# Moving GpSimd's two-operand arithmetic to VectorE in a two-layer hybrid diffusion block

## The chip, the cores and the metric

The kernel runs on one core of a Trainium2 chip. A core has TensorE (PE, with its weight loads shown apart as PEld), VectorE (DVE), ScalarE (ACT), GpSimd (POOL) and SyncE (SP), each with a queue of its own that runs strictly in order, and DMA queues. The metric is the device time of one execution in microseconds (us), the median of several runs. A profiled execution is one more run, with its own time.

## What is computed

Two layers over 512 latent tokens and 256 context tokens of width 1024. Each layer projects its input to four token mixers (grouped-query attention with 2-D rotary, neighbourhood attention, Fourier mixing, a complex diagonal state-space scan), normalizes and joins them, projects them out, and runs a SwiGLU:

```
h = _rmsnorm(x, g_norm1) * (1.0 + sc1) + sh1
aq, ak, av, dq, dk, dv, fin, sin_ = _split_proj(h @ w_in)
...
o_a, oc_a = _gqa_mixer(aq, ak, av, caq, cak, cav, att_q_gain, att_k_gain, rope, need_ctx)
o_d, oc_d = _na_mixer(dq, dk, dv, cdq, cdk, cdv, na_q_gain, na_k_gain, na_rel_bias, need_ctx)
o_f = _fourier_mixer(fin, w_fourier)
o_s, oc_s = _s5_mixer(sin_, csin, ssm_lam_re, ssm_lam_im, ssm_log_dt, ssm_b_re, ssm_b_im,
                      ssm_c_re, ssm_c_im, ssm_d, w_glu, b_glu, need_ctx)
o = _group_norm(jnp.concatenate([o_a, o_d, o_f, o_s.astype(o_a.dtype)], axis=-1), g_group)
x = x + ga1 * (o @ w_out)
h2 = _rmsnorm(x, g_norm2) * (1.0 + sc2) + sh2
x = x + ga2 * _swiglu(h2, w_ff1, w_ff3, w_ff2)
```

The rotary step multiplies each head's halves by cosines and sines. The state-space mixer's powers of a_bar and its products with B and C are made on the chip as tables.

## The kernel before

Tokens lie on the free axis, channels on the 128 partitions. All large products are made in three matmuls from halves in fp32r: a weight tile `raw` (128x1024 f32, or 128x768 for the value projection) comes by a DMA on SP's queue, ScalarE casts it to `hi`, and GpSimd takes `lo = raw - hi` (`weights`, L222 to L235). `mm3` (L237) then adds hi times hi, hi times lo, and lo times hi, in that order. There are four buffers of `hi`, four of `lo` and two of `raw`; a buffer comes free when TensorE has done with its weights, or for `raw`, when both halves are made. 178 such tiles go through in one execution.

The order of the work on each engine is set by a scheduler that plays the program against a timeline of its own; weights stand at high priority. Each engine's queue then holds that order, and an instruction at its head that waits holds up all that stands behind it.

Stages, by the profile's time axis: from 0 to about 143 us the first layer's state-space tables (`tables`, L424 to L680: small DVE steps on tiles `sm`, then per m and direction the tiles `bg`, `bd`, `ot`, `o`, `gt`, `g`, and the rotation table `ro`, L661 to L666), its modulation and norm (`norm_apply`, L320, tiles `xa`, `h`) and its first projections; from 143 to 255 us rotary (`rope`, L914) and the scan (`s5`, L707, tiles `zt`, `hst`); to 450 us attention and Fourier; to 1065 us the output projection and the feed-forward (`dense`, L1261), which near its end, from 850 us, also makes the tables of the second layer; to 1145 us the norm between the layers; to 1295 us projections and scan of the second layer; to 1430 us its attention; and to 1834 us its output projection and feed-forward.

In the feed-forward each of 22 slices f takes two weight tiles (w1 and w3), silu on ScalarE, a product on DVE (`sg`, L1332) and a split into `gh` (ScalarE) and `gl` (DVE, L1337). After every three or four slices `down` adds their product with w2 to x (`update`, L1248). The psum tiles `psD` of these products are two in layer one, four in layer two.

In the tables GpSimd makes one product of every pair that DVE then adds or subtracts (`q2`, `q3`, `o2` as tile `o`, `g2` as tile `g`), one-operand copies (L594, L668), memsets and the loads `sbg`, `sbd`, `scd` of layer one. In `rope` GpSimd multiplies by the cosines. GpSimd's queue also issues DMAs of `s5` and of the Fourier part.

Of the kernel before, what the change touches and what calls it, by code (L numbers as in the profile page):

```python
# [18 lines left out]
P = 128  # L19
D = 1024  # L20
KT = 8
SEQ = 512
# [26 lines left out]
C_COS, C_SIN = 461, 973  # L49
# [134 lines left out]
class _Core:  # L184
# [37 lines left out]
    def weights(self, src, shape):  # L222
        nc = self.nc
        n = int(np.prod(shape))
        with self.tc.high_priority():
            hi = self.whi.tile([P, n], F32R, name="hi")
            raw = self.raw.tile([P, n], F32, name="raw")
            lo = self.wlo.tile([P, n], F32R, name="lo")
            pat = " ".join("abcd"[:len(shape)])
            nc.sync.dma_start(raw, src.rearrange(f"p {pat} -> p ({pat})") if len(shape) > 1 else src)  # L230
            nc.scalar.copy(hi, raw)  # L231
            nc.gpsimd.tensor_sub(lo, raw, hi)  # L232
        if len(shape) == 1:
            return hi, lo
        return tuple(t.rearrange("p (a b) -> p a b", b=shape[1]) for t in (hi, lo))  # L235
# [188 lines left out]
    def tables(self, l, tp, t2, role, nm, gate=None):  # L424
        nc, a = self.nc, self.a
        v, gp = nc.vector, nc.gpsimd
# [109 lines left out]
        for k in (1, 2, 4):  # L536
            o = slice(k + 1, 2 * k + 1)
            br, bi = (pw[:, i, k:k + 1].broadcast_to([P, k, M]) for i in range(2))
# [17 lines left out]
        ng = 16 // nm  # L556
# [3 lines left out]
        for m in range(nm):  # L560
# [3 lines left out]
            for d in range(2):  # L564
                with self.tc.issue_after(gate(m, d).ins) if gate and gate(m, d) else ExitStack():
# [4 lines left out]
                    def rev(ap):  # L570
                        return ap[:, ::-1] if d == 1 else ap

                    sbg = t2.tile([P, 2, np2, 16], F32, name="sbg", bufs=sb)
                    ld.dma_start(sbg, a["sbg"][:, :, q, ps2])
                    sbd = t2.tile([P, 2, ng, 16], F32, name="sbd", bufs=sb)
# [4 lines left out]
                    q2 = t2.tile([P, 2, np2, 16], F32, name="q2")  # L580
                    f8r, f8i = (t[:, c8].unsqueeze(2).broadcast_to([P, np2, 16]) for t in (fr, fi))
                    v.tensor_mul(bg[:, 0], sbg[:, 0], f8r)
                    gp.tensor_mul(q2[:, 0], sbg[:, 1], f8i)
                    v.tensor_mul(bg[:, 1], sbg[:, 1], f8r)
                    gp.tensor_mul(q2[:, 1], sbg[:, 0], f8i)
                    v.tensor_sub(bg[:, 0], bg[:, 0], q2[:, 0])
                    v.tensor_add(bg[:, 1], bg[:, 1], q2[:, 1])
                    bd = t2.tile([P, ng, 2, 16], F32, name="bd")
                    q3 = t2.tile([P, ng, 16], F32, name="q3")
                    f6r, f6i = (t[:, c16].unsqueeze(2).broadcast_to([P, ng, 16]) for t in (fr, fs))  # L590
                    v.tensor_mul(bd[:, :, 0], sbd[:, 0], f6r)
                    gp.tensor_mul(q3, sbd[:, 1], f6i)
                    v.tensor_add(bd[:, :, 0], bd[:, :, 0], q3)
                    gp.tensor_copy(bd[:, :, 1], bd[:, :, 0])  # L594
                    ot = t2.tile([P, ng, 9, 16], F32, name="ot", tag="w", bufs=wb)
# [1 line left out]
                    for dst, ci in ((ot, 0), (o2, 1)):  # L597
                        pv = rev(p12[:, ci, :, c16]).rearrange("p s g -> p g s").unsqueeze(3)
                        cv = scd[:, ci].unsqueeze(2)
                        (v if ci == 0 else gp).tensor_tensor(dst, pv.broadcast_to([P, ng, 9, 16]),  # L600
                                                             cv.broadcast_to([P, ng, 9, 16]), op=ALU.mult)
                    v.tensor_add(ot, ot, o2)
                    osl = ot[:, :, 0:8] if d == 1 else ot[:, :, 1:9]
# [14 lines left out]
                    else:  # L618
# [5 lines left out]
                    pr, pi = (rev(pw[:, i, 0:8, c8]).rearrange("p s g -> p g s").unsqueeze(3).broadcast_to(shp)  # L624
                              for i in range(2))
                    br, bi = (bg[:, i].unsqueeze(2).broadcast_to(shp) for i in range(2))
                    g2 = t2.tile(shp, F32, name="g2")
                    v.tensor_mul(gt[:, 0], pr, br)
                    gp.tensor_mul(g2, pi, bi)
                    v.tensor_sub(gt[:, 0], gt[:, 0], g2)  # L630
                    g3 = t2.tile(shp, F32, name="g3")
                    v.tensor_mul(gt[:, 1], pr, bi)
# [281 lines left out]
    def rope(self, t):  # L914
        nc = self.nc
        sw = self.xn.tile([P, NT], F32, name="xn")
        nc.vector.stream_shuffle(sw[:, :SEQ], t[:, :SEQ], list(range(16, 32)) + list(range(16)))
        nc.gpsimd.tensor_mul(t[:, :SEQ], t[:, :SEQ], self.cst[:, C_COS:C_COS + SEQ])
        nc.vector.tensor_mul(sw[:, :SEQ], sw[:, :SEQ], self.cst[:, C_SIN:C_SIN + SEQ])
        nc.vector.tensor_add(t[:, :SEQ], t[:, :SEQ], sw[:, :SEQ])  # L920

# [531 lines left out]
```

## Time and profile before

| | us |
|---|---|
| median of 3 runs | 1827.36 (1827.08 to 1835.4) |
| the profiled execution | 1835.55, of which span 1833.8 |
| TensorE busy | 1725.8 (94%) |
| VectorE busy | 969.5 (53%) |
| ScalarE busy | 527.2 (29%) |
| GpSimd busy | 558.6 (30%) |

Times in the rows below are microseconds from the span's start. A busy TensorE counts matmuls that are pipelined, with modelled ends. "a <- b" in a list of waits means that a waited and that b's end released it. In the chain of work each step is followed back to what released it.

### The profile page before, as it was taken

How to read it: one execution, taken by the hardware profiler on the slowest of the kernel's cores; microseconds unless marked ns; L12 is line 12 of the kernel's file. 1: busy time of each engine (PE TensorE's matmuls, PEld its weight loads, DVE VectorE, ACT ScalarE, POOL GpSimd, SP SyncE). 2: the span in 40 equal slices, each digit the busy share in tenths (PEclk: the TensorE clock that was granted, in tenths of full speed). 3: DMA queues.
4: the chain of work that ended last, by engine and by line, in shares of the span. 5: the costliest groups of instructions: out<-in, count | busy, mean ns of one | idle time of the engine just before them, and what ended most of it. 6: DMA issues, size and time to landing. Idle time of an engine off the chain costs nothing.

```text
span 1833.8 us, 25688 instructions
## 1 busy us (share of the span) xinstructions
PE 1725.8 (94%) x10142; PEld 1395.3 (76%) x10142; DVE 969.5 (53%) x2259; ACT 527.2 (29%) x852; POOL 558.6 (30%) x360
## 2 busy tenths in 40 slices
PE   5899999898999999999899998989999999999999
PEld 2667877566878888888678877778767787787887
DVE  7988535572177445446956346265666632232332
ACT  2422234452241211121121223323444432222221
POOL 4553200201221322231643512423111244344442
PEclk7999989999999999999899998989999999999999
DMA  8355340414135434343342332332322123233222
GB/s 337 103 155 165 128 167 24 167 53 182 38 125 151 127 127 153 107 154 110 106 110 75 106 112 81 132 110 89 114 64 64 47 92 93 77 107 103 93 92 81
DMA packets 83065, 207.25 MB, mean 113 GB/s; under 512 B 15360, under 2 KB 35968, under 8 KB 82816
## 3 DMA queue, kind: packets, MB, share of 16 engines
q1 hardware_dynamic: 54160, 160.44, 26.9%
q0 software_dynamic: 7824, 29.38, 4.8%
q10 hardware_dynamic: 20960, 15.78, 2.8%
q8 instruction: 80, 1.31, 0.3%
q14 instruction: 41, 0.34, 0.1%
HBM read 185.68 MB, written 21.99 MB: 113 GB/s over the span
## 4 chain that ended last, share of the span: by engine, by line
PE 76%; DVE 15%; issue 4%; ACT 2%; POOL 1%; DMA 1%; ACTq 0%; DVEq 0%; POOLq 0%
PE psD L241 54%; PE psD L703 4%; PE psS L932 3%; PE psT L241 2%; PE psQ L979 1%; PE psQ L990 1%; PE psT L376 1%; PE psS L801 1%; POOL lo L232 1%; PE psT L856 1%; PE psQ L1045 1%; DVE ro L662 1%; PE psQ L1030 1%; PE psT L278 1%; PE psT L1067 1%
## 5 line engine op out<-in xcount | busy, mean ns | idle before, releaser
L232 POOL TENSOR_TENSOR lo<-raw,hi 128x1024 fp32r<-128x1024 f32 (+1 forms) x178 | 432.2, 2434 | 875.5 <-ACT hi L231 875.2
L241 PE MATMUL psD<-big,hi 128*128 128x512 f32 (+1 forms) x2368 | 605.9, 360 | 12.2 <-ACT big L331 5.7
L241 PEld LDWEIGHTS psD<-big,hi 128*128 128x128 f32 x2368 | 399.8, 191 | 88.1 <-ACT big L331 8.1
L231 ACT CAST hi<-raw 128x1024 fp32r<-128x1024 f32 (+1 forms) x178 | 184.2, 1039 | 774.5 <-PE psD L241 466.6
L241 PE MATMUL psD<-big,lo 128*128 128x512 f32 (+1 forms) x1184 | 368.2, 359 | 1.2 <-POOL lo L232 1.2
L241 PEld LDWEIGHTS psD<-big,lo 128*128 128x128 f32 x1184 | 202.9, 191 | 38.4 <-POOL lo L232 2.7
L1332 DVE TENSOR_TENSOR sg<-sg,psD 128x768 f32<-128x768 f32 (+1 forms) x44 | 36.1, 820 | 308.8 <-PE psD L241 300.5
L241 PE MATMUL psD<-gh,hi 128*128 128x512 f32 (+1 forms) x528 | 163.6, 359 | 4.9 <-DVE xb L1248 4.7
L241 PE MATMUL psD<-gl,hi 128*128 128x512 f32 (+1 forms) x528 | 165.8, 360 | 0.0
L241 PE MATMUL psD<-gh,lo 128*128 128x512 f32 (+1 forms) x528 | 163.6, 358 | 0.0
L1248 DVE SCALAR_TENSOR_TENSOR xb<-psD,mod,xb 128x512 f32<-128x512 f32 (+1 forms) x112 | 64.7, 613 | 114.9 <-PE psD L241 114.8
L1337 DVE TENSOR_TENSOR gl<-sg,gh 128x768 fp32r<-128x768 f32 (+1 forms) x44 | 99.2, 2254 | 39.5 <-ACT gh L1335 39.5
L407 DVE CUSTOM_DVE_ANT_0 junk<-wmt,cb,pcol 128x1024 f32<-128x1024 f32 x64 | 97.1, 1517 | 27.3 <-DMA wmt<-in_wmodT 26.2
L241 PEld LDWEIGHTS psD<-gh,hi 128*128 128x128 f32 x528 | 89.5, 189 | 24.4 <-DVE xb L1248 8.5
L241 PEld LDWEIGHTS psD<-gh,lo 128*128 128x128 f32 x528 | 90.1, 189 | 16.6 <-issue 0.2
L241 PEld LDWEIGHTS psD<-gl,hi 128*128 128x128 f32 x528 | 89.8, 189 | 15.8 <-issue 0.4
L1248 DVE SCALAR_TENSOR_TENSOR xq<-psD,mod,xq 128x512 f32<-128x512 f32 (+1 forms) x64 | 42.2, 682 | 78.6 <-PE psD L241 78.6
L932 PE MATMUL psS<-k,q 64*128 64x256 f32 (+1 forms) x432 | 78.2, 336 | 3.4 <-DVE mx L1019 3.0
L241 PE MATMUL psD<-h,hi 128*128 128x512 f32 (+1 forms) x288 | 76.2, 350 | 4.2 <-ACT h L331 2.7
L932 PEld LDWEIGHTS psS<-k,q 64*128 64x128 f32 x432 | 58.1, 195 | 23.6 <-issue 9.1
L241 PEld LDWEIGHTS psD<-h,hi 128*128 128x128 f32 x288 | 50.7, 194 | 15.4 <-ACT h L331 3.2
L241 PE MATMUL psD<-on,hi 128*128 128x256 f32 (+1 forms) x176 | 51.6, 331 | 1.3 <-ACT on L1081 1.3
(396 smaller groups left out, 2494.5 us busy)
## 6 DMA issues: line engine op xcount, KB each, us to landing
raw<-in_w_ff SPq DMA_DIRECT2D x132, 512.0 KB, 3.5
wmt<-in_wmodT SPq DMA_DIRECT2D x48, 512.0 KB, 3.6
wm<-in_wmod SPq DMA_DIRECT2D x28, 512.0 KB, 6.0
raw<-in_winT SPq DMA_DIRECT2D x18, 512.0 KB, 3.6
room<-in_wmod SPq DMA_DIRECT2D x12, 512.0 KB, 11.4
nab<-in_nab SPq DMA_DIRECT2D x8, 640.0 KB, 4.2
rot<-trot POOLq DMA_DIRECT2D x8, 576.0 KB, 6.0
cf<-in_four POOLq DMA_DIRECT2D x8, 520.0 KB, 4.9
```

The lines of the kernel that those rows point to most:

```text
L231: nc.scalar.copy(hi, raw)
L232: nc.gpsimd.tensor_sub(lo, raw, hi)
L241: nc.tensor.matmul(o, lhsT=lhs[i], rhs=rhs[j][..., s], start=start and n == 0, stop=stop and n == 2)
L278: self.nc.tensor.matmul(dst, lhsT=src, rhs=self.ident, start=True, stop=True)
L376: nc.tensor.matmul(ps[32 * j:32 * j + 32], lhsT=self.cvec[:, k], rhs=ws[k // 2][:, k % 2], start=half == 0, stop=half == 1)
L407: nc.vector.tensor_tensor_reduce(junk, w, cb[:, i], 1.0, self.pcol[1][:, PC_B + f:PC_B + f + 1], op0=ALU.mult, op1=ALU.add, accum_out=mod[ ...
L662: v.tensor_mul(er[:, :, :, o], er[:, :, :, s], bcr)
L703: nc.tensor.matmul(ps, lhsT=h[i][:, k, tk], rhs=w[j][:, k % per], start=k == 0 and q == 0, stop=k == KT - 1 and q == 2)
L932: self.nc.tensor.matmul(dst, lhsT=q2[i][h, qc], rhs=view(k2[j][h]), start=n == 0, stop=n == 2)
L1248: self.nc.vector.scalar_tensor_tensor(x[:, m, sl], ps[:, sl], gate[:, m, i:i + 1], x[:, m, sl], op0=ALU.mult, op1=ALU.add)
L1332: nc.vector.tensor_mul(sg, sg, pp[1])
L1337: marks.append(nc.vector.tensor_sub(gl, sg, gh))
```

## The change

Every GpSimd instruction with two tensor operands is issued on VectorE instead: the low half of each weight tile, five products in each pass of the tables, and the cosine product of the rotary step. Operands and results are the same. GpSimd keeps copies, memsets and DMA issues.

```
-            nc.gpsimd.tensor_sub(lo, raw, hi)
+            nc.vector.tensor_sub(lo, raw, hi)
...
-                    gp.tensor_mul(q2[:, 0], sbg[:, 1], f8i)
+                    v.tensor_mul(q2[:, 0], sbg[:, 1], f8i)
...
-                    gp.tensor_mul(q2[:, 1], sbg[:, 0], f8i)
+                    v.tensor_mul(q2[:, 1], sbg[:, 0], f8i)
...
-                    gp.tensor_mul(q3, sbd[:, 1], f6i)
+                    v.tensor_mul(q3, sbd[:, 1], f6i)
...
-                        (v if ci == 0 else gp).tensor_tensor(dst, pv.broadcast_to([P, ng, 9, 16]),
+                        v.tensor_tensor(dst, pv.broadcast_to([P, ng, 9, 16]),
...
-                    gp.tensor_mul(g2, pi, bi)
+                    v.tensor_mul(g2, pi, bi)
...
-        nc.gpsimd.tensor_mul(t[:, :SEQ], t[:, :SEQ], self.cst[:, C_COS:C_COS + SEQ])
+        nc.vector.tensor_mul(t[:, :SEQ], t[:, :SEQ], self.cst[:, C_COS:C_COS + SEQ])
```

The scheduler orders all engines anew. VectorE's queue, first norm of layer one (`h`, `xa`: norm_apply; `mod`, `gsc`: modulation), before:

```order
L332 SCALAR_TENSOR_TENSOR h_269<-xa,mod_87,h_268 128x512
L329 SCALAR_TENSOR_TENSOR xa<-xa,gsc_0_88,psS 128x256
L332 SCALAR_TENSOR_TENSOR h_269<-xa,mod_87,h_268 128x256
L329 SCALAR_TENSOR_TENSOR xa<-xa,gsc_0_88,psS 128x256
L332 SCALAR_TENSOR_TENSOR h_269<-xa,mod_87,h_268 128x256 x2
L385 TENSOR_TENSOR mod_87<-psD,pcol_85 128x8
L332 SCALAR_TENSOR_TENSOR h_269<-xa,mod_87,h_268 128x256
L354 SCALAR_TENSOR_TENSOR gsc_0_88<-mod_87,pcol_85 128x8
L329 SCALAR_TENSOR_TENSOR xa<-xa,gsc_0_88,psS 128x512 x3
```

and now:

```order
L385 TENSOR_TENSOR mod_87<-psD,pcol_85 128x8
L332 SCALAR_TENSOR_TENSOR h_269<-xa,mod_87,h_268 128x512
L329 SCALAR_TENSOR_TENSOR xa<-xa,gsc_0_88,psS 128x256
L232 TENSOR_TENSOR lo<-raw,hi 128x1024
L332 SCALAR_TENSOR_TENSOR h_269<-xa,mod_87,h_268 128x256
L329 SCALAR_TENSOR_TENSOR xa<-xa,gsc_0_88,psS 128x256
L354 SCALAR_TENSOR_TENSOR gsc_0_88<-mod_87,pcol_85 128x8
L232 TENSOR_TENSOR lo<-raw,hi 128x1024
L332 SCALAR_TENSOR_TENSOR h_269<-xa,mod_87,h_268 128x256 x2
L329 SCALAR_TENSOR_TENSOR xa<-xa,gsc_0_88,psS 128x512 x3
```

The third and fourth low halves now stand between the steps of this norm, where GpSimd ran them beside it.

VectorE's queue, the last direction of the first layer's scan (`zt`, `hst`: state of the scan), before:

```order
L757 TENSOR_TENSOR zt<-psS,rot 128x384
L758 TENSOR_TENSOR zt<-zt 128x384
L759 TENSOR_TENSOR zt<-zt 128x384
L765 SCALAR_TENSOR_TENSOR zt<-rot,zt 128x384 x2
```

and now:

```order
L757 TENSOR_TENSOR zt<-psS,rot 128x384
L758 TENSOR_TENSOR zt<-zt 128x384
L232 TENSOR_TENSOR lo<-raw,hi 128x1024
L759 TENSOR_TENSOR zt<-zt 128x384
L765 SCALAR_TENSOR_TENSOR zt<-rot,zt 128x384
L232 TENSOR_TENSOR lo<-raw,hi 128x1024
L765 SCALAR_TENSOR_TENSOR zt<-rot,zt 128x384
```

Two low halves, which need ScalarE's `hi`, now stand ahead of three steps of the scan.

VectorE's queue, a turn from `down` to the next slices in the second layer's feed-forward (`xq`: update, `sg`, `gl`: slice), before:

```order
L1337 TENSOR_TENSOR gl<-sg,gh 128x512
L1248 SCALAR_TENSOR_TENSOR xq<-psD,mod_92,xq 128x512 x8
L1332 TENSOR_TENSOR sg<-sg,psD 128x512
L1337 TENSOR_TENSOR gl<-sg,gh 128x512
L1332 TENSOR_TENSOR sg<-sg,psD 128x512
```

and now:

```order
L1337 TENSOR_TENSOR gl<-sg,gh 128x512
L1248 SCALAR_TENSOR_TENSOR xq<-psD,mod_92,xq 128x512 x7
L232 TENSOR_TENSOR lo<-raw,hi 128x1024 x2
L1248 SCALAR_TENSOR_TENSOR xq<-psD,mod_92,xq 128x512
L232 TENSOR_TENSOR lo<-raw,hi 128x1024 x3
L1332 TENSOR_TENSOR sg<-sg,psD 128x512
```

The low halves of the next slice's two weights stand ahead of the last update, three more ahead of the first product.

## Rows read from the trace of the kernel before

**Rows 1.** The page's first part: busy time, share and count of each engine.
```profile
PE 1725.8 (94%) x10142; PEld 1395.3 (76%) x10142; DVE 969.5 (53%) x2259; ACT 527.2 (29%) x852; POOL 558.6 (30%) x360
```

**Rows 2.** The page's fourth part: the chain of work by engine.
```profile
PE 76%; DVE 15%; issue 4%; ACT 2%; POOL 1%; DMA 1%; ACTq 0%; DVEq 0%; POOLq 0%
```

**Rows 3.** VectorE's timeline: start, duration, instruction.
```profile
15.39 0.20 DVE L466 TENSOR_TENSOR sm<-sm,sm 128x48 f32<-128x48 f32 x1
15.51 2.37 DVE L516 TENSOR_TENSOR sm<-sm 128x48 f32<-128x48 f32 x1
17.80 2.39 DVE L491 SCALAR_TENSOR_TENSOR sm<-sm,sm 128x48 f32<-128x48 f32 x1
...
60.45 2.33 DVE L354 SCALAR_TENSOR_TENSOR gsc<-mod,pcol 128x8 f32<-128x8 f32 x1
...
118.57 2.45 DVE L662 TENSOR_TENSOR ro<-ro 128x64 f32<-128x64 f32 x1
...
1809.06 2.43 DVE L1337 TENSOR_TENSOR gl<-sg,gh 128x512 fp32r<-128x512 f32 x1 [0.69 <-ACT gh L1335]
```

**Rows 4.** GpSimd's timeline at the first and third low halves.
```profile
15.38 4.74 POOL L232 TENSOR_TENSOR lo<-raw,hi 128x1024 fp32r<-128x1024 f32 x2 [8.64 <-ACT hi L231]
...
57.86 4.89 POOL L232 TENSOR_TENSOR lo<-raw,hi 128x1024 fp32r<-128x1024 f32 x2 [8.51 <-ACT hi L231]
```

**Rows 5.** The chain in order of time: start, length, what.
```profile
15.59 2.29 DVE sm L516
...
876.57 2.35 DVE sm L510
...
897.81 2.38 DVE q L663
...
901.29 5.15 POOL o L600
...
1293.38 3.30 DVE gr L250
```

**Rows 6.** Groups by form, VectorE and GpSimd: count, then busy us, mean ns.
```profile
L600 DVE TENSOR_TENSOR ot<-sm,scd 128x1152 f32<-128x1152 f32 x4 | 5.4, 1346 | 0.0
L1337 DVE TENSOR_TENSOR gl<-sg,gh 128x512 fp32r<-128x512 f32 x22 | 52.5, 2386 | 19.5 <-ACT gh L1335 19.5
...
L232 POOL TENSOR_TENSOR lo<-raw,hi 128x1024 fp32r<-128x1024 f32 x170 | 416.0, 2453 | 873.9 <-ACT hi L231 873.6
...
L232 POOL TENSOR_TENSOR lo<-raw,hi 128x768 fp32r<-128x768 f32 x8 | 16.2, 2022 | 1.7 <-ACT hi L231 1.6
```

**Rows 7.** Busy time by stage: engines with counts, then PEclk, DMA share, GB/s.
```profile
0.00:143.00 143.00, 114.09 (x624) 77.01 (x625) 120.51 (x364) 42.56 (x64) 72.84 (x67) 0.89 0.58 203
...
450.00:850.00 400.00, 392.83 (x2229) 337.26 (x2229) 196.45 (x281) 90.42 (x106) 111.99 (x47) 0.99 0.39 125
850.00:1065.00 215.00, 199.30 (x1131) 168.25 (x1130) 139.04 (x464) 38.71 (x50) 96.06 (x83) 0.95 0.32 93
...
1145.00:1295.00 150.00, 140.90 (x942) 118.99 (x943) 75.28 (x184) 48.49 (x78) 52.19 (x48) 0.94 0.36 115
...
1430.00:1834.00 404.00, 394.52 (x1812) 319.99 (x1811) 128.10 (x169) 105.44 (x143) 159.01 (x66) 0.99 0.28 89
```

**Rows 8.** Waits of TensorE from 850 to 1065 us.
```profile
PE psT L611 <- DVE ot L602: 12.4, 3, 8.0
```

**Rows 9.** Waits of TensorE's weight loads from 1430 us on.
```profile
PEld psD L241 <- POOL lo L232: 2.5, 3, 0.8
```

**Rows 10.** VectorE and ScalarE in the scan's last direction.
```profile
208.15 0.55 DVE L758 TENSOR_TENSOR zt<-zt 128x384 f32<-128x384 f32 x1
...
212.66 3.18 DVE L782 TENSOR_TENSOR hst<-zt 64x380 f32<-64x380 f32 x2
...
210.84 2.09 ACT L231 CAST hi<-raw 128x1024 fp32r<-128x1024 f32 x2 [0.99 <-issue]
```

## Prediction

> **What bounds the kernel now.** I read the page's busy times first: TensorE is busy 94% of the span, VectorE 53%, GpSimd 30% [rows 1]. So most of the time is matmuls, and an engine change can only win what TensorE idles, 1833.8 - 1725.8 = 108 us, and what it runs at a lower clock. The chain of work says who takes that: TensorE 76% of the span, VectorE 15%, GpSimd itself only 1% [rows 2]. By the chain alone GpSimd's arithmetic costs next to nothing; what matters is what VectorE's 15% consist of.
>
> That is seen in VectorE's timeline. A 128x48 step takes 0.20 us at 15.39; the next two, of the same size, take 2.37 and 2.39 [rows 3], and they are the ones that run while GpSimd makes two low halves, from 15.38 for 4.74 us [rows 4]. At 60.45 an 8-element step takes 2.33 us, again inside a pair of low halves (57.86 for 4.89). A VectorE step with two operands in SBUF thus waits until GpSimd's two-operand step is over. I compared every VectorE step in the timeline with the fastest tenth of the same instruction and shape (for `gl` of L1337, which nearly always meets a low half, with 0.70 and 0.96 us, the time of L1332 at the same size): 112 steps are longer by over 0.15 us, from L516 at 15.51 to L1337 at 1809.06 [rows 3], together 156 us. In the chain in order of time 42 VectorE steps are over 0.2 us too long, from L516 at 15.59 to L250 at 1293.38 [rows 5], together 61 us: 17.1 before 143 us, 0.8 to 255, 2.1 to 450, 1.8 to 850, 23.2 to 1065, 4.3 to 1145, 11.3 to 1295, none behind. The price is paid where VectorE leads, the tables, norms and scans, not in the feed-forward.
>
> **What the change adds.** Each moved instruction becomes a VectorE step that competes with nobody but still takes its turn. No row shows `lo` on VectorE. The nearest is L600, two SBUF operands in f32, 128x1152 in 1346 ns [rows 6], or 1.17 ns an element: 1.20 us for 128x1024, 0.90 for 128x768. From above, L1337, the same subtraction into fp32r at 128x512, takes 2386 ns beside GpSimd [rows 6], and GpSimd's own 2.45 us bounds it too; both hold the wait that goes, so I take 1.20. 170 of 1.20 and 8 of 0.90 are 211 us. The tables' five products have 1152 + 512 + 128 + 2 x 64 = 1920 elements in each of 4 passes of layer one, half that in 8 passes of layer two: 9.0 us each. Six rotary products of 512 elements: 3.6. VectorE gets 224 + 9 = 233 us and loses 156, and ends near 969.5 + 77, or 57%. It doesn't become the bound on the mean; in stages it may.
>
> **Stage by stage**, since the gain of one is capped by what TensorE idles there:
> - 0 to 143 us: VectorE is busy 120.5 of 143 us [rows 7] and leads. 20 of the 112 long steps lie here, the last at 118.57 [rows 3], together 28.7 us. Added: nine low halves of 1024 and one of 768 (11.7) and the tables (9.0). 28.7 - 20.7 = 8.0 us gained, of 28.9 that TensorE idles.
> - 143 to 255 us: the two scan steps at 212.66 lose about 2 x 0.53 us of work to 3.18 [rows 10], and rotary no longer crosses to GpSimd. But the new order puts two low halves ahead of these steps, and `hi` is not there before 211.9 (210.84 + half of 2.09), while VectorE reaches that point at 208.7 [rows 10]: it would wait there. One for the other: 0.
> - 255 to 850 us: 2.1 + 1.8 = 3.9 us of the chain's long steps; TensorE idles 7.2 in the feed-forward part [rows 7], and the low halves fit into a VectorE that is busy 196 of 400 us. 3.9 gained.
> - 850 to 1065 us: the second layer's tables. 23.2 us of long steps on the chain, and GpSimd's product `o`, itself held up to 5.15 us [rows 5]; TensorE waits 12.4 us for `ot`, 8.0 in one piece [rows 8]. Back on the chain come the tables' 9.0 us and some six of the 21 low halves (7.2), those between the table steps. 28.3 - 16.2 = 12.1, below the 15.7 us that TensorE idles [rows 7].
> - 1065 to 1145 us: 4.3 less two low halves in the norm's chain: 1.9.
> - 1145 to 1295 us: 11.3 less rotary (1.8) and four low halves of 0.90 and two of 1.20 (6.0): 3.5, of 9.1 idle [rows 7].
> - 1430 us on: TensorE waits for a low half at three turns, 2.5 us in all, at most 0.8 each [rows 9]. A low half in 1.20 instead of 2.45 us covers each: 2.5. The other stalls of this stage hit `gl`, which `down` needs only slices later: nothing.
>
> Sum: 8.0 + 0 + 3.9 + 12.1 + 1.9 + 3.5 + 2.5 = 31.9 us. Not all of it will arrive. The scheduler has made a new order, an estimate of mine is that a third goes to what is next latest (ScalarE's casts, DMAs of the tables, and waits like the one at 208.7), so I forecast 21 us. Against the profiled execution: 1835.55 - 21 = 1814.5; that execution lies 8.2 us over the median, so for the median 1827.4 - 21 = **1806 us**, by itself 1796 to 1818.
>
> [...]
>
> **Rivals.**
> 1. *VectorE was the bound in the first stage and the long steps are its own.* It is busy 84% there; if nothing comes back, the added 20.7 us, 9.0 for the second tables and 3.6 rotary all show: 1827 + 33 = 1860. Against it: the same line at 0.20 and 2.39 us, with starts that agree with GpSimd's to 0.2 us. Chance 0.03.
> 2. *Masked.* TensorE's queue is full, and what stalls VectorE is late for nobody: only direct waits for low halves go, 2.5 us and a little of the tables: 1823. For it: the chain is inferred, and where VectorE waits for DMA or ScalarE next the gain stops. Against it: the 8.0 us in one piece. Chance 0.16.
> 3. *The wait moves into VectorE's queue.* A low half needs `hi`, `hi` a buffer that TensorE frees; on GpSimd that wait held up nobody (873.9 us of idle [rows 6]). On VectorE it holds scan, softmax and norm steps, and TensorE waits for these. Price, from the place at 208.7: 3.2 us of wait and 1.2 of work. 39 of the 178 low halves lie in the mixers of both layers (before 450 us, and 1145 to 1430). The sum of 31.9 us is spent from seven such places on; with ten of them the kernel is slower, 1827 + 44 - 32 = 1839. Chance 0.12.
> 4. *More.* All 32 us arrive, and TensorE, no longer starved, keeps its clock: in the first stage 0.89 of full is granted, 0.95 in 850 to 1065 [rows 7]. At 0.95 and 0.97 its busy 114 and 199 us would shrink by 7 and 4: 1827 - 32 - 11 = 1784. Chance 0.19.
>
> That the change doesn't do what it says is a part of case 2: GpSimd keeps one-operand copies (L594, L668), which may still block a VectorE step, but they are 18 short ones.
>
> **How the numbers follow.** Forecast 0.50, rivals 0.03, 0.16, 0.12, 0.19. A difference of 0.5%, 9.1 us, is about what a measurement of this kernel can tell from no change: faster is below 1818.2, slower above 1836.5. Faster: 0.49 of the forecast, all of rival 4, a little of 2: 0.70. Same: nearly all of 2, a bit of the forecast and of 3: 0.16. Slower: 0.14 (rival 1, nearly all of 3, and a small rest). The range reaches from 1785, nearly to rival 4, over rival 2 to 1828; rivals 1 and 3 and the tail below, under 0.2, stay out.
>
> **What would show it.** Right: no VectorE step of 0.2 us that takes over 1 us; `gl` at 128x512 near 0.7; `lo` on VectorE near 1.2 us; TensorE idle less in 0 to 143 and in the second tables, where the 8 us wait of L611 is gone; VectorE busy near 1045 us. Wrong: VectorE waiting for `hi` of L231 ahead of scan or table steps, with TensorE waiting for VectorE (rival 3); or all that and the same end (rival 2). The forecast falls if `lo` takes over 2 us on VectorE, or if the new order sets table matmuls ahead of feed-forward ones by more than VectorE can meet.

## The result

The changed kernel takes 1784.93 us (median of 4 runs, 1781.54 to 1788.35) where the kernel before, on the same chip, takes 1827.22. The ratio is 0.9762, 95% interval 0.9732 to 0.9792: faster by 42 us between the medians, or 2.4%. The forecast was 1806 us, in a range of 1785 to 1828. The result lies just below the range: the sign and the cause were right, and the gain was twice the forecast, since two terms of the sum failed (the part on why, below).

One execution of a kernel differs from another mainly in the clock that TensorE is granted (before, on all chips: 1817.49 us at a mean of 0.974, 1840.87 us at 0.964; the changed kernel's means lie between 0.976 and 0.985), and the two profiled ones lie on opposite sides of their medians: 1835.55 and 1781.54 us. So 54.0 us part the two traces, and 42 the medians; the 12 us between are read as clock in what follows, not as an effect of the change; a single trace of before can't show that. One execution of E1 below, 2761.43 us at a mean granted clock of 0.554, is in a slow state and left out of its ratio.

The page of the changed kernel, its busy times and its chain by engine, beside [rows 1, 2]:

```profile
PE 1702.4 (96%) x10142; PEld 1379.4 (78%) x10142; DVE 1017.7 (57%) x2503; ACT 529.3 (30%) x852; POOL 68.0 (4%) x116
...
PE 87%; DVE 8%; issue 2%; ACT 1%; DMA 1%; POOL 0%; SPq 0%; DVEq 0%; ACTq 0%
```

VectorE has more to do and yet its part of the chain is halved. TensorE's busy time fell by 23 us although it does the same 10142 matmuls. VectorE's groups by form, beside [rows 6]:

```profile
L232 DVE TENSOR_TENSOR lo<-raw,hi 128x1024 fp32r<-128x1024 f32 x170 | 207.1, 1223 | 173.0 <-ACT hi L231 171.4
...
L1337 DVE TENSOR_TENSOR gl<-sg,gh 128x768 fp32r<-128x768 f32 x22 | 21.0, 953 | 0.3 <-ACT gh L1335 0.3
L1337 DVE TENSOR_TENSOR gl<-sg,gh 128x512 fp32r<-128x512 f32 x22 | 15.1, 686 | 0.0
...
L232 DVE TENSOR_TENSOR lo<-raw,hi 128x768 fp32r<-128x768 f32 x8 | 7.6, 954 | 0.1
```

A low half takes 1.22 us on VectorE, and `gl` at 128x512 went from 2.39 to 0.69 us. Counted as the prediction did it (each step against the fastest tenth of its kind, over 0.15 us), the 112 long VectorE steps with 156 us have become one with 0.6 us. That way counts the rows of the timeline that hold a single step; with the steps that a row merges counted too, one by one, it is 122 with 171 us before and three with 1.6 now.

TensorE's time by stage, first before, then after. The cuts are the ends of the same VectorE steps in both kernels (the first rotary step of L917, the first maximum of L972, the 1st, 14th, 22nd and 23rd product of L1332), but for the last cut but one: at 1316.8 stands the 31st maximum of L972, at 1269.0 the 33rd. Columns: stretch, its length, TensorE's busy time with its matmuls, granted clock, DMA share, GB/s.

```profile
0.00:143.30 143.30, 114.39 (x627) 0.89 0.58 203
143.30:259.20 115.90, 105.57 (x783) 0.98 0.42 147
259.20:538.10 278.90, 260.89 (x1787) 0.95 0.28 97
538.10:845.20 307.10, 304.08 (x1732) 1.00 0.45 141
845.20:1081.00 235.80, 220.10 (x1248) 0.96 0.33 96
1081.00:1316.80 235.80, 216.06 (x1378) 0.94 0.34 111
1316.80:1476.40 159.60, 152.27 (x1091) 0.98 0.16 50
1476.40:1833.80 357.40, 352.41 (x1508) 1.00 0.30 95
```

```profile
0.00:132.50 132.50, 109.14 (x637) 0.92 0.58 201
132.50:241.90 109.40, 102.55 (x772) 0.98 0.51 179
241.90:512.70 270.80, 256.56 (x1789) 0.96 0.29 100
512.70:819.40 306.70, 303.31 (x1730) 1.00 0.44 141
819.40:1033.60 214.20, 211.16 (x1249) 1.00 0.36 105
1033.60:1269.00 235.40, 224.57 (x1424) 0.95 0.34 111
1269.00:1424.50 155.50, 144.17 (x1049) 1.00 0.17 52
1424.50:1779.80 355.30, 350.98 (x1505) 1.00 0.31 95
```

Length less busy time is what TensorE idles. Set against the prediction's terms (the sixth and seventh stretch are taken together, since the cut between them is not at the same step):

| stage before, us | gain forecast (idle) | idle gone | busy time gone |
|---|---|---|---|
| 0 to 143 | 8.0 | 5.6 | 5.3 |
| 143 to 259 | 0 | 3.5 | 3.0 |
| 259 to 538 | 2.1 | 3.8 | 4.3 |
| 538 to 845 | 1.8 | -0.4 | 0.8 |
| 845 to 1081 | 12.1 | 12.7 | 8.9 |
| 1081 to 1476 | 5.4 | 4.9 | -0.4 |
| 1476 on | 2.5 | 0.7 | 1.4 |
| sum | 31.9 | 30.7 | 23.3 |

The idle time that went is, to 4%, the sum worked out ahead of the discount. In part that is luck, since errors of single stages cancel. The rest is matmuls that run faster, and one place of that can be seen. TensorE in stretches of 5 us in the first tables, before and then after:

```profile
95.00:100.00 5.00, 3.56 (x23) 1.00 0.11 25
100.00:105.00 5.00, 3.49 (x20) 0.70 0.85 229
105.00:110.00 5.00, 5.00 (x28) 0.62 0.88 283
```

```profile
90.00:95.00 5.00, 5.00 (x34) 1.00 0.50 143
95.00:100.00 5.00, 5.00 (x36) 1.00 0.36 104
100.00:105.00 5.00, 5.00 (x34) 1.00 0.27 108
```

Before, TensorE waits for `ot` of L602 for 3.0 us in one piece, which lie half in the first and half in the second stretch, the clock falls, and the third, busy throughout, still has 0.62. After, nothing idles there and the clock stays at 1.00.

### The profile page after: what moved, and what is told of

The parts are those of the page before. It is cut to its first block, busy times and chain, and to the rows that moved or that the text cites. A ratio compares the mean times of both kernels' runs of the same rounds, so it can differ in the third digit from the quotient of the medians.

```text
span 1779.8 us, 25610 instructions
## 1 busy us (share of the span) xinstructions
PE 1702.4 (96%) x10142; PEld 1379.4 (78%) x10142; DVE 1017.7 (57%) x2503; ACT 529.3 (30%) x852; POOL 68.0 (4%) x116
## 4 chain that ended last, share of the span: by engine, by line
PE 87%; DVE 8%; issue 2%; ACT 1%; DMA 1%; POOL 0%; SPq 0%; DVEq 0%; ACTq 0%
PE psD L241 62%; PE psD L703 4%; PE psS L932 4%; PE psT L241 2%; PE psQ L979 2%; PE psQ L990 1%; DVE lo L232 1%; PE psT L376 1%; PE psQ L1045 1%; PE psT L856 1%; PE psT L278 1%; PE psS L801 1%; PE psQ L1030 1%; PE psT L1067 1%; PE psT L265 1%
## 5 line engine op out<-in xcount | busy, mean ns | idle before, releaser
L241 PE MATMUL psD<-big,hi 128*128 128x512 f32 (+1 forms) x2368 | 601.1, 357 | 11.6 <-ACT big L331 7.7
L241 PEld LDWEIGHTS psD<-big,hi 128*128 128x128 f32 x2368 | 394.5, 189 | 88.7 <-ACT big L331 10.2
L241 PE MATMUL psD<-big,lo 128*128 128x512 f32 (+1 forms) x1184 | 364.3, 355 | 0.0
L232 DVE TENSOR_TENSOR lo<-raw,hi 128x1024 fp32r<-128x1024 f32 (+1 forms) x178 | 214.7, 1211 | 173.1 <-ACT hi L231 171.4
L1332 DVE TENSOR_TENSOR sg<-sg,psD 128x768 f32<-128x768 f32 (+1 forms) x44 | 36.1, 821 | 151.9 <-PE psD L241 151.9
L407 DVE CUSTOM_DVE_ANT_0 junk<-wmt,cb,pcol 128x1024 f32<-128x1024 f32 x64 | 82.1, 1283 | 29.1 <-DMA wmt<-in_wmodT 27.3
L241 PE MATMUL psD<-on,lo 128*128 128x256 f32 (+1 forms) x176 | 50.5, 324 | 0.0
```

The costliest lines, as they stand in the source:

```text
L232: nc.vector.tensor_sub(lo, raw, hi)
L241: nc.tensor.matmul(o, lhsT=lhs[i], rhs=rhs[j][..., s], start=start and n == 0, stop=stop and n == 2)
L407: nc.vector.tensor_tensor_reduce(junk, w, cb[:, i], 1.0, self.pcol[1][:, PC_B + f:PC_B + f + 1], op0=ALU.mult, op1=ALU.add, accum_out=mod[ ...
L1332: nc.vector.tensor_mul(sg, sg, pp[1])
```

## Experiments

Twelve experiments ran, one of them (E9) the changed kernel again. The ratios are to the kernel before on the same chip. "Long steps" are counted as above; "idle" is the profiled span less TensorE's busy time; "half clock" is the time at a granted clock of 0.50 that the mean granted clock of the span amounts to, (1 - clock) x 2 x span, with the clock unrounded: of 1833 stretches of 1 us in the trace of before, 1698 are at 1.00, 102 at 0.50 and 33 between, of 1779 of the changed kernel 1697, 62 and 20. Both are of one execution each.

| kernel | ratio (95%) | long steps, us | idle, us | half clock, us |
|---|---|---|---|---|
| before | 1 | 156 | 108 | 121 |
| changed | 0.9762 (0.9732 to 0.9792) | 0.6 | 77 | 72 |
| E1 low halves alone | 0.9787 (0.9734 to 0.9840) | 17 | 81 | |
| E2 tables and rotary alone | 0.9844 (0.9810 to 0.9878) | 140 | 94 | 90 |
| E3 useless subtraction on GpSimd | 1.0091 (1.0062 to 1.0120) | 158 | 120 | 138 |
| E4 useless copy on GpSimd | 0.9790 (0.9756 to 0.9824) | 65 | 86 | 82 |
| E5 useless memset on GpSimd | 0.9772 (0.9726 to 0.9817) | 9 | 80 | 101 |
| E6 feed-forward low halves on GpSimd | 0.9730 (0.9679 to 0.9781) | 72 | 78 | 41 |
| E7 the other low halves on GpSimd | 0.9887 (0.9843 to 0.9931) | 64 | 103 | 85 |
| E8 last copies off GpSimd | 0.9685 (0.9646 to 0.9723) | 0 | 82 | 55 |
| E9 changed kernel again | 0.9746 (0.9721 to 0.9771) | 0.9 | 79 | 66 |
| E10 E6 and E8 together | 0.9742 (0.9710 to 0.9775) | 70 | 76 | 55 |
| E11 six short stalls | 0.9825 (0.9799 to 0.9851) | 1.0 | 90 | 58 |
| E12 six long stalls | 1.0011 (0.9994 to 1.0028) | 0.6 | 117 | 99 |

(E1's profiled execution records a third level, 0.95, for its first half and 0.959 on average, though its matmuls of `psD` from `big` and `hi` at 128x512 take 397 ns on average, as the changed kernel's do, 398 ns at 0.980; so its half-clock time is left out.)

**Theories.** A: VectorE's steps are held by GpSimd's two-operand steps, and the stalls on the path of TensorE are what the change won back. B: the tables' own chain, whose products were slow on GpSimd. C: the stalls were hidden, and the gain is the low half itself, 1.22 us instead of 2.45, or the new order.

E3, E5 and E9 keep the order of the changed kernel (VectorE's 2503 steps, ScalarE's 852 and the 10142 matmuls follow one another alike), and E11 and E12 keep it but for the products that they turn round. In E1, E2, E4, E6, E7, E8 and E10 the scheduler made an order anew, so their times hold that too.

### E1 and E2: one part of the change alone

E1:
```diff
-            nc.gpsimd.tensor_sub(lo, raw, hi)
+            nc.vector.tensor_sub(lo, raw, hi)
```


> The kernel before with one line of the change: the 178 low halves on VectorE, table products and rotary cosine still on GpSimd. Of the 112 long VectorE steps of before, 77 with 122.5 of 156 us overlap a low half more than any other GpSimd step. Theory A (VectorE steps were held by GpSimd's two-operand steps, and that is what the 42 us were): most of the gain comes with this line alone, 1790 to 1803 us; the long steps left lie at table products, under 40 us in total; TensorE still waits for `ot` of L602 in the second tables, as GpSimd's product is still there. Theory B (the gain is the tables' own shorter chain): 1815 to 1825. Theory C (the gain is that a low half takes 1.22 instead of 2.45 us, the stalls were hidden): 1790 to 1803 as well; the third run tells it from A.

E2 is the rest of the change: the tables' products and the rotary cosine on VectorE, this line left as it was.

> The rest of the change alone: table products and rotary cosine on VectorE, the 178 low halves still on GpSimd. Theory A: the low halves go on holding VectorE's steps, and hold the 9 + 9 us of new table steps too; only the waits for the tables' products and the 25 us of long steps beside them go: 1808 to 1822 us, with over 100 us of long steps left. Theory B (the tables' own chain): 1785 to 1795.

E1 came as theory A said in its time and its long steps, E2 better than it said: 28 us gained where at most 20 were expected, with 140 of the 156 us of long steps still there. The parts don't add up (39 and 28 us alone, 43 together, by the ratios, in intervals of some 10 and 6 us each way); E1's interval holds the changed kernel's ratio, so nothing shows that the tables' products add to it. In E1 the first layer's tables go on waiting for GpSimd, for a copy, as a row of TensorE's waits has it (who waits for whom: us in all, times, longest):

```profile
PE psS L611 <- POOL bd L594: 8.1, 2, 4.6
```

The wait for `ot` of L602 that theory A expected there is not in E1's trace: in the second tables, where before has 8.0 us in one piece [rows 8], E1's matmuls have no wait before L611, though GpSimd makes all of their products, and E2 still has one of 8.2 us, though GpSimd makes none (E7, below, has one of 5.9). So that wait goes with the low halves. In E2 the profile names no releaser for it, and `gl` is held as before:

```profile
PE psT L611 <- issue: 8.2, 1, 8.2
L1337 DVE TENSOR_TENSOR gl<-sg,gh 128x512 fp32r<-128x512 f32 x22 | 52.5, 2388 | 18.9 <-ACT gh L1335 18.9
```

E2 is 28 us faster all the same, so microseconds of stall are not microseconds of time. What can be said: idle fell by 27 us in E1, by 14 in E2 and by 31 with both, so some 10 us of it go by either part alone; that a table product on GpSimd and a low half are in each other's way there is a guess. The other half of E2's gain is, in the traces, busy time (15.8 us). Theory B alone is out: without the low halves a third of the gain is missing.

### E3, E4, E5: the contention alone

The changed kernel, with one useless GpSimd step for each weight tile; its result is read by nobody. E3:
```diff
+        self.jk = pool("jk", 1)
...
             nc.vector.tensor_sub(lo, raw, hi)
+            jk = self.jk.tile([P, 1024], mybir.dt.bfloat16, name="jk")
+            nc.gpsimd.tensor_sub(jk[:, :n], hi, hi)
```


> The changed kernel with 178 useless GpSimd steps, one for each weight tile, as large as the low half was: a subtraction of `hi` from `hi` (two operands in SBUF, result in bf16, read by nobody). Nothing waits for them but the buffer of `hi`. All of the change's order, of its shorter low half and of its tables stays. Theory A: the long VectorE steps come back (over 80 of them, over 100 us, at 2.4 us for 0.2), now also among the low halves on VectorE themselves, and with them most of the 42 us or more: 1815 to 1850. Theory C (the shorter low half, or the new order, made the gain): within 5 us of the changed kernel, 1782 to 1790.

E4 and E5 have other steps in its place, E4 the first line, E5 the other two:
```diff
+            nc.gpsimd.tensor_copy(jk[:, :n], hi)
...
+            nc.gpsimd.tensor_copy(jk[:, :1], hi[:, :1])
+            nc.gpsimd.memset(jk[:, :n], 0.0)
```


> The same with a GpSimd copy of one operand (`hi`, 128x1024 to bf16) for each weight tile in the place of the subtraction. If only GpSimd's second operand holds VectorE: 1782 to 1790 and no long steps. If any GpSimd step that reads SBUF does, the long steps come back as with the subtraction, each as long as such a copy lasts: 1800 to 1850. That the kernel before kept one-operand copies on GpSimd, and L594 and L668 have one long step each of 0.6 and 0.3 us beside them, speaks a little for the second.

> The same place as the useless GpSimd steps before, but the step only writes: a copy of one column of `hi`, so that it comes at the same time, then a memset of the 128x1024 bf16 tile. If GpSimd holds VectorE by what it reads, the long steps don't come back and the time stays within 4 us of the changed kernel: 1781 to 1789 us (0.974 to 0.979 of before). If any GpSimd work of this size does it (or the mere extra semaphores on `hi`): 1792 or more, as with the copy.

The groups by form of the useless step, the low half and `gl`, in E3, in E4 and in E5 (their line numbers lie 1 to 4 higher than the changed kernel's):

```profile
L235 POOL TENSOR_TENSOR jk<-hi 128x1024 bf16<-128x1024 f32 x170 | 443.1, 2606 | 871.0 <-ACT hi L232 863.3 <-ACT wt L622 4.5
L233 DVE TENSOR_TENSOR lo<-raw,hi 128x1024 fp32r<-128x1024 f32 x170 | 283.9, 1675 | 122.6 <-ACT hi L232 120.6
L1340 DVE TENSOR_TENSOR gl<-sg,gh 128x512 fp32r<-128x512 f32 x22 | 50.7, 2305 | 0.0
```

```profile
L235 POOL CAST jk<-hi 128x1024 bf16<-128x1024 f32 x170 | 301.5, 1773 | 981.1 <-ACT hi L232 979.8
L233 DVE TENSOR_TENSOR lo<-raw,hi 128x1024 fp32r<-128x1024 f32 x170 | 238.7, 1409 | 148.5 <-ACT hi L232 146.0
L1340 DVE TENSOR_TENSOR gl<-sg,gh 128x512 fp32r<-128x512 f32 x22 | 33.5, 1524 | 0.0
```

```profile
L233 DVE TENSOR_TENSOR lo<-raw,hi 128x1024 fp32r<-128x1024 f32 x170 | 206.9, 1222 | 175.4 <-ACT hi L232 173.3
L236 POOL MEMSET jk<- 128x1024 bf16 x170 | 162.1, 953 | 9.9
L235 POOL CAST jk<-hi 128x1 bf16<-128x1 f32 x178 | 148.8, 836 | 1014.5 <-ACT hi L232 1012.8
...
L1341 DVE TENSOR_TENSOR gl<-sg,gh 128x512 fp32r<-128x512 f32 x22 | 15.1, 685 | 0.0
```

E3 settles theory C: with the short low half, the tables and the order of the changed kernel in place, useless subtractions bring back 158 us of long steps and cost 60 us (1.0091 less 0.9762), all of the gain and more. The copy does less (`gl` 1.52 us; about 5 us in all, and the intervals overlap), the memset nothing: `gl` is 0.685 us again and the ratio that of the changed kernel. The GpSimd of E5 is busy 375.5 us and that of E4 375.9; in E5 168 us of that are memsets, 23 of the 44 `gl` overlap one, and none is longer for it. So it is not GpSimd's being busy but what it reads. E4's forecast of 1800 us or more was too high: the long steps came back, at about half of E3's length, and cost little.

Against the changed kernel's 0.686 us, `gl` at 128x512 is longer by 1.62 us in E3, 0.84 in E4 and 0.00 in E5.

### E6 and E7: where a stall costs

A flag of `weights` sends some low halves back to GpSimd; the rest of the changed kernel stays. E6:
```diff
-            nc.vector.tensor_sub(lo, raw, hi)
+            (nc.gpsimd if pool else nc.vector).tensor_sub(lo, raw, hi)
...
+                    ws = [self.weights(a[nm][l, f], (KT, P), l == 1 or f < 14) for nm in ("w_ff1", "w_ff3")]
...
+                w2 = [self.weights(a["w_ff2"][l, f], (D,), l == 1 or f < 14) for f in fs]
```
E7 has the flag the other way round.

> The changed kernel, but the 108 low halves of the feed-forward stages in which TensorE leads (layer one up to f = 13, all of layer two) are back on GpSimd; the other 70 stay on VectorE. In the kernel before these stages (538 to 845 and from 1476 us) hold 45 of the 112 long steps and 68 of their 156 us, but only 1.8 us of the chain's 61, and TensorE idles 8.0 us in them. Theory A (a stall costs only where VectorE leads): the 68 us come back and the time hardly moves, 1785 to 1793 us (0.976 to 0.980 of before). Rival (stalls cost in proportion to their length wherever they stand): 68/156 of 42 us lost, 1803 (0.986).

> The complement: the 70 low halves of the mixers, of the norms and of layer one's feed-forward from f = 14 (beside the second tables) on GpSimd, the 108 others on VectorE. Theory A: here is the price; with all 178 on GpSimd the kernel took 0.9844 of before, and this one should be near it, 0.982 to 0.986 (1797 to 1804). Rival (in proportion to their number): 70/178 of the way from 0.9762 to 0.9844, 0.9794 (1791).

E6 keeps 72 us of long steps and is no slower; E7 has 64 us of them and loses 23 (0.9887 against 0.9762), half the gain. (With merged steps counted one by one it is 75 and 72 us.) How large E7's price is stays loose: E2, with the same 70 low halves and the 108 others on GpSimd, took 0.9844, which is 15 us. E6's feed-forward stages (538 to 845 and from 1476 in before):

```profile
506.80:815.50 308.70, 305.68 (x1733) 1.00 0.43 140
1410.70:1768.00 357.30, 352.38 (x1507) 1.00 0.30 95
```

They are 2 us longer than in the changed kernel each, so 72 us of stalls cost some 4 us there. Theory A's step "the price is paid where VectorE leads, not in the feed-forward" holds. E6 came out below its forecast (0.976 to 0.980), with an interval that holds it. E7 came out above its forecast (0.982 to 0.986), but its interval reaches into it; in it the waits of `hst` are back:

```profile
PE psS L801 <- DVE hst L784: 7.0, 2, 4.1
```

### E8, E9, E10: a kernel that is faster still?

E8 takes the last arithmetic from GpSimd, E9 repeats the changed kernel on the chip of E10, and E10 is E6 with E8's two lines:
```diff
-                    gp.tensor_copy(bd[:, :, 1], bd[:, :, 0])
+                    v.tensor_copy(bd[:, :, 1], bd[:, :, 0])
...
-                gp.tensor_copy(ro[:, :, 2], cd8(rho).unsqueeze(3).broadcast_to([P, 2, np2, 96]))
+                nc.scalar.copy(ro[:, :, 2], cd8(rho).unsqueeze(3).broadcast_to([P, 2, np2, 96]))
```


> The changed kernel with GpSimd's last arithmetic taken from it too: the 12 copies of L594 (1.5 us each on GpSimd, of 128x64 and 128x128 elements) on VectorE, the 6 of L668 on ScalarE. TensorE waits for L594 5.5 us before L611, ScalarE longer. Theory: a few us faster than the changed kernel, 1776 to 1783 (0.972 to 0.975 of before), the two long VectorE steps beside L668 gone, and most of it in the first tables. If the wait only passes to the step before it: 1784 to 1787.

> The changed kernel once more, on the same chip as the three others of this set, so that these are compared with it directly: 1780 to 1790 us, a mean granted clock of 0.977 to 0.981.

> Both steps that seemed to help, together: GpSimd's copies of L594 and L668 on VectorE and ScalarE, and the 108 low halves of the feed-forward stages in which TensorE leads on GpSimd. Theory: a low half on GpSimd costs nothing in those stages (TensorE idles 3.0 and 5.0 us there against 3.4 and 4.3 in the changed kernel), and VectorE is free for what the mixers need next; the copies give what they gave alone, 0.9685: 1763 to 1775 us (0.964 to 0.971 of before). If the split gave nothing (its interval reaches that of the changed kernel): the same as the copies alone, 0.9685. If the two collide: over 0.973.

E8's 0.9685 is the lowest ratio of all and below its forecast (0.972 to 0.975); its interval ends 0.0009 below that of the changed kernel in the second row of the table, and within that of E9. But its idle is not lower (82 us against 77 and 79); what is lower is its time at half clock. E10 holds the same two lines, misses its forecast (0.964 to 0.971) and is level with the changed kernel on the same chip, 0.9742 and 0.9746. So either the copies are worth nothing and E8 was lucky, or they are worth some 10 us and E10's low halves on GpSimd cost as much; the intervals of E8 and E10 overlap, and it stays open. By its stages the second is unlikely: E10's two feed-forward stages take 306.8 and 357.4 us, where the changed kernel has 306.7 and 355.3.

### E11 and E12: what an idle of TensorE costs

In layer two's feed-forward, where TensorE idles next to nothing, the down projection sums from the newest `gh` on, so TensorE must wait six times; E12 makes the wait longer with the second piece:
```diff
-                    for i, f in enumerate(fs):
+                    for n in range(len(fs)):
+                        i = len(fs) - 1 - n if l == 1 else n
...
-                                 gt[i], i == 0, i == len(fs) - 1)
+                                 gt[i], n == 0, n == len(fs) - 1)
```
```diff
+                    if l == 1 and f == fs[-1]:
+                        for _ in range(8):
+                            nc.vector.tensor_scalar(sg, sg, 1.0, None, op0=ALU.mult)
                     hi = nc.scalar.copy(gh, sg)
```


> The changed kernel with the down projection of layer two summed from the last f to the first, so that TensorE, six times, has to wait for the newest `gh`: Silu 0.59, product 0.69, cast 0.62 us, with hops about 2.1 us each, in a stage where the granted clock is 1.00 and TensorE idles 4.3 of 355 us. If an idle of TensorE costs just its length: idle 16 to 18 us there, TensorE's busy time unchanged at 351, 12 to 13 us slower in all. If the clock falls after each such stall, as after 95 to 105 us of the kernel before: busy time 5 to 10 us longer too, and 18 to 25 us slower.

> The same six stalls, made longer by eight more VectorE steps on `sg` (times 1.0, 128x512) ahead of the cast: an estimate of 2.4 to 5.5 us more for each, so 4.5 to 7.6 us and 27 to 46 us of idle in all. If an idle costs just its length: that and no more, with a clock of 1.00 and 351 us busy. If the clock falls after a long idle: mean granted clock of the stage 0.97 or lower and busy time 5 to 15 us longer.

The stage in E11 and in E12, to be set against the last row of the changed kernel above:

```profile
1416.80:1788.50 371.70, 357.05 (x1505) 0.99 0.29 91
```

```profile
1420.40:1826.20 405.80, 364.79 (x1505) 0.95 0.26 83
```

The same 1505 matmuls. E11: idle 4.3 to 14.7 us, busy time up by 6.1. E12: idle 4.3 to 41.0, busy time up by 13.8. In these two traces an idle cost itself and some 0.4 (E12) to 0.6 (E11) of itself again. In E12 the clock fell at each of the six stalls: the stage's mean of 0.95 amounts to some 41 us at half clock, and the 0.63 and 0.69 in the two stretches of 5 us from 1525 us on, around the end of the stall shown below, to 6.8, a sixth of it. In E11 it fell behind the third and the fifth only (0.75 and 0.68 in the 5 us that follow, 1.00 behind the four others):

```profile
1585.00:1590.00 5.00, 5.00 (x18) 0.75 0.29 102
```

A mean of 0.99 over 371.7 us is some 7 us at half clock. From before to the changed kernel the time at half clock fell from 121 to 72 us, by 49, and the busy time by 23.3 us, 0.48 of that. At this share the 7 us are an estimated 3.4 of E11's 6.1 us; where the rest comes from is not shown. One of the six stalls, TensorE's timeline in E12 (start, duration, instruction, and in brackets the idle before it):

```profile
1522.28 0.39 PE L241 MATMUL psD<-big,lo 128*128 128x512 f32 x1
1528.87 2.07 PE L241 MATMUL psD<-gh,hi 128*128 128x512 f32 x4 [6.20 <-ACT gh L1338]
1530.74 0.63 PE L241 MATMUL psD<-gl,hi 128*128 128x512 f32 x1
...
1533.23 0.39 PE L241 MATMUL psD<-gl,hi 128*128 128x512 f32 x1
```

A matmul of 0.39 us takes 0.63 after the wait, until 1533. In time, E11 lost 14 us against E9 (0.9825 less 0.9746) and E12 48. E11 lies between its two expectations (12 to 13, and 18 to 25): its busy time rose as much as the clock theory said, but the clock fell behind two stalls and not behind each, and the stalls were 1.6 us long instead of 2.1.

## Why the prediction was right or wrong

- **The stall.** Right. GpSimd's two-operand step holds VectorE's [rows 3, 4]; E3 makes it at will (`gl` at 128x512 takes 2.31 us) and E5 takes it away (0.69).
- **What the change adds.** Right. The low half was forecast at 1.20 and 0.90 us and takes 1.22 and 0.95. VectorE ends at 1018 us, 57%; 1045 was forecast. More went than the 156 us: 969.5 + 233 - 1018 is 185, of which the long steps in merged rows, not counted then, are 15.
- **Where it costs.** Right: the mixers, norms and tables, not the feed-forward (E6, E7).
- **The sum.** 31.9 us of idle were forecast and 30.7 went. Stage by stage it is less good, but the errors cancel, which is luck. The first stage was over-sized (8.0 against 5.6) and so was the last (2.5 against 0.7): [rows 9] are waits of the weight loads, and at these three turns TensorE's matmuls idled 1.2 us, which now are gone. TensorE's waits before:

```profile
PE psD L241 <- POOL lo L232: 1.2, 3, 0.4
```

The zero of 143 to 255 us was wrong (3.5 went): before, TensorE waited 4.6 us for a low half ahead of L801, and now the low halves in the scan do not wait for `hi`, as VectorE's timeline of the changed kernel shows, with no idle ahead of any row:

```profile
198.42 0.55 DVE L758 TENSOR_TENSOR zt<-zt 128x384 f32<-128x384 f32 x1
198.88 1.22 DVE L232 TENSOR_TENSOR lo<-raw,hi 128x1024 fp32r<-128x1024 f32 x1
200.02 0.56 DVE L759 TENSOR_TENSOR zt<-zt 128x384 f32<-128x384 f32 x1
200.49 0.95 DVE L765 TENSOR_TENSOR_SCAN zt<-rot,zt 128x384 f32<-128x384 f32 x1
201.35 1.21 DVE L232 TENSOR_TENSOR lo<-raw,hi 128x1024 fp32r<-128x1024 f32 x1
```

- **The discount, the first step that failed.** The prediction took 10.9 us off its 31.9 ("an estimate of mine is that a third goes to what is next latest") with no row behind it; the traces lose 1.2. What might have been next latest was there (171 us of VectorE's waits for `hi` at L232), and little of it reached TensorE. In places a next latest did: at 725 and 829 us of the changed kernel VectorE waits 2.6 us for the modulation's DMA ahead of four updates (before, two of the four stood ahead of that wait), and TensorE 2.3 and 2.2 us for the updated `xb`. In the stage of 538 to 845 us its waits for `xb` grew from 2.95 to 3.39 us, which is the -0.4 there, where 1.8 was forecast. VectorE's timeline:

```profile
723.05 1.28 DVE L407 CUSTOM_DVE_ANT_0 junk<-wmt,cb,pcol 128x1024 f32<-128x1024 f32 x1 [2.65 <-DMA wmt<-in_wmodT]
...
724.26 2.19 DVE L1248 SCALAR_TENSOR_TENSOR xb<-psD,mod,xb 128x512 f32<-128x512 f32 x4
```

- **The clock, the second.** The prediction names it at its start among what can be won, but the sum has no term for it: it stood only in rival 4, with a chance of 0.19, as something that might come on top. In the traces 23.3 us of busy time went with 30.7 of idle, and by the medians, if the idle is the same in each execution (77 and 79 us in two profiles of the changed kernel; before has one), 42.3 less 30.7 is 11.6 us. So where the forecast had 31.9 - 10.9 + 0 = 21, the runs have 30.7 + 11.6 = 42.3. Rival 4 put 32 and 11 us together and gave 1784; 1784.93 was measured. That it is so near is in part luck: its 11 us were those of the first stage and the second tables, where 14.2 went in the traces (5.3 and 8.9).
- **The cap at the second tables.** The 15.7 us of idle were held to be all that could be won there; 21.6 went (12.7 and 8.9), since the clock rose from 0.96 to 1.00.
- **Rivals 1 and 2** are out: VectorE's long steps were not its own (E3), and more than the direct waits went. **Rival 3** did not happen: low halves wait for `hi` 76 times on VectorE, 8.6 us at the longest, but TensorE's matmuls wait for no low half, its weight loads 1.4 us in all (7.5 before), and its waits for `hst` (6.9 us before) are gone. The low halves' own time is felt: they are 1% of the chain, and at 1071 us two of them, 2.35 us, stand ahead of the norm's steps while TensorE waits 2.25 us for the norm's `big`.

## What to carry to other kernels

When an engine of the chain has steps of one shape with two very different durations, line up the long ones with GpSimd's instructions that read SBUF (158 us of long steps beside E3's subtractions, 65 beside E4's copies, 9 beside E5's memsets), and then ask stage by stage whether TensorE idles for them: 72 us of such stalls cost some 4 us beside the feed-forward's matmuls, and 64 us in the mixers and tables 15 to 23 us, up to half of the change's gain. Price an idle of TensorE at more than its length where the granted clock falls behind it (by 0.4 to 0.6 of it in E11 and E12), as a term of the sum. Don't take a share off a sum without a row that says who is late next.

## What was not expected of the hardware

- One-operand GpSimd copies hold VectorE's two-operand steps too: `gl` 1.52 us beside a 128x1024 copy, 2.31 beside a subtraction, 0.69 beside a memset.
- GpSimd is held in its turn: E5's copy of a single column takes 0.18 us at the least and 0.84 on average, with VectorE's low half running from the same `hi`; L594's copy of 128x128 takes 0.29 us at 48.01 us of before and 3.3 us on average in E1.
- Executions with the same idle can differ in time at half clock: E5, at 80 us of idle, has 101 us of it, E6, at 78, has 41; the changed kernel has 72 and 66 in two executions. What sets that was not tried.
